# Gate projections by Strassen's seven products, w_out in 512-column halves, and two conditioning blocks in another order

## The chip, the cores and the metric

The kernel runs on one core of a Trainium2 chip. The metric is the device time of one execution in microseconds (us), the median of several runs. TensorE is called PE here, VectorE DVE, ScalarE ACT, GpSimd POOL, and SyncE SP. All DMAs of the kernel are issued from SP's queue.

## The reference

Two layers over 1024 latent tokens and 256 context tokens, each of width 1024. The change touches the projection of the gates `g`, the merge and the output projection:

```python
h = _rms(x) * (1.0 + scale) + shift               # scale, shift, gate: s_c @ w_ada[l] + b_ada[l]
fa, za, u, vs, zb, q, k, va, zc, g = _split_proj(h @ w_in[l])
# three mixers: Fourier (ya), gated spatial mixing (yb), windowed attention (yc)
ga, gb, gc = jnp.split(jax.nn.sigmoid(g), 3, axis=-1)       # each [tokens, 1024]
merged = ga * (ya @ w_pa) + gb * (yb @ w_pb) + gc * (yc @ w_pc)
x = x + gate * (merged @ w_out)
```

The context tokens go through the same layer with their own conditioning in layer 0, and give only keys and values in layer 1.

## The kernel before

**Numbers.** Every float32 product is made of three fp32r products: an operand is split into a high part (a cast on ACT, `whi`, `hh`) and a low part (a subtraction on DVE, `wlo`, `hl`), and `mm3` adds high times high, high times low and low times high in PSUM. So a projection of 128 output columns over 1024 inputs for one token group is 8 x 3 matmuls. Latents are in two groups of 512 tokens, "0" and "1"; the context is group "C" with 256. `H[g]` holds the normalised input of a group as eight [128, tokens] high and eight low tiles; later the same name holds the merged values.

**Stages of a layer.** Attention with side work; the Fourier mixer with the products of `w_pc`; spatial mixing (`sgu`) with the products of `w_pa` (`products`, results stored to DRAM as P); the gates; the output phase. Some gate blocks are computed ahead, in the stages before (`ahead`, results stored as T): four 512-token blocks in layer 0, eight in layer 1, besides those of the context.

**Gates (`gates`, L663 on).** For each of eight column blocks j and three branches b, one projection of 24 matmuls 512 wide for each latent group: 44 such blocks are left in layer 0, 40 in layer 1. The weights come as one [128, 8, 128] tile, cast (L212) and subtracted (L213) 1024 columns at a time. ACT takes the tanh, DVE forms (tanh + 1) * P (`add`, L673 and L676), POOL adds it to the merged tile M (L677). The products of `w_pb` are made in the same loop, into PSUM, and used from there. Merged latents go through DRAM; the merged context goes straight into `H["C"]`.

**Conditioning.** Next to the gates, DVE also multiplies rows of `w_ada` by the conditioning vectors and accumulates them (`ada_dve`, L192 and L196, 256 columns at a time): twelve items of two column blocks in layer 0, each 16 instructions, and four items of 8 instructions in layer 1. A tiny matmul (L200) sums over partitions.

**Output phase (`out_phase`).** For a token group, four quarters of `w_out` of 256 columns; for each, 24 matmuls per 128 tokens, then DVE multiplies by the gate (L927) and POOL adds to x (L929). Group order in layer 0: C, 0, 1. Then `modulate` prepares the next layer.

**Start.** Four blocks of layer 0's conditioning (`ada_rows`, 512 columns each): one at a time by eight fp32 matmuls on PE, and one with the sums on DVE.

**What sets the order.** The program is written in order with "fill" generators that place PE work between steps; a scheduler then moves instructions on each engine by its own timeline, and each engine runs its list strictly in that order.

Of the kernel before, what the change touches and what calls it, by code (L numbers as in the profile page):

```python
# [66 lines left out]
def trunk_kernel(ctx: ExitStack, tc: tile.TileContext, a: dict, out: bass.AP):  # L67
# [109 lines left out]
    def ada_dve(l, jb, nv, pool):  # L177

        raws = []
        for half in range(2):  # L180
            raw = pool.tile([128, 4, 256], F32, "araw", bufs=2)
            src = a["w_ada"][l, half * 512:(half + 1) * 512, jb * 128:jb * 128 + 256]
            nc.sync.dma_start(raw, src.rearrange("(k p) c -> p k c", p=128))
            raws.append(raw)

        def finish():
            acc = pool.tile([128, nv, 256], F32, f"aacc{nv}")
            for k in range(8):
                for v in range(nv):
                    sc = scol[:, k, v:v + 1]  # L190
                    if k == 0:
                        ins = DVE.tensor_scalar(acc[:, v, :], raws[0][:, 0, :], sc, None, ALU.mult)  # L192
                        if v == 0:
                            tc.keep_in_program_order(ins)
                    else:
                        DVE.scalar_tensor_tensor(acc[:, v, :], raws[k // 4][:, k % 4, :], sc, acc[:, v, :], ALU.mult, ALU.add)  # L196
            pa = bank("o")
            for i in range(2):
                for v in range(nv):
                    PE.matmul(pa[:, 2 * i + v:2 * i + v + 1], acc[:, v, i * 128:(i + 1) * 128], ones[:, 0:1], start=True, stop=True)  # L200
            for i in range(2):
                DVE.tensor_scalar(adac[l][:, jb + i, 0:nv], pa[:, 2 * i:2 * i + nv], bada[l][:, jb + i:jb + i + 1], None, ALU.add)

        return finish


    def granule(src, shape):
        raw = wp.tile(shape, F32, "raw", bufs=2)
        nc.sync.dma_start(raw, src)
        hi = wp.tile(shape, F32R, "whi", bufs=5)  # L210
        lo = wp.tile(shape, F32R, "wlo", bufs=5)
        ACT.copy(hi, raw)  # L212
        DVE.tensor_tensor(lo, raw, hi.bitcast(F32), ALU.subtract)  # L213
        return hi, lo

    def w_cm(l, c0):

        return granule(a["w_in"][l, :, c0:c0 + 128].rearrange("(k p) c -> p k c", p=128), [128, KC, 128])

    def w_tm(w, c0):  # L220

        r = []
        for half in range(2):
            src = w[half * 512:(half + 1) * 512, c0:c0 + 256].rearrange("(k p) c -> p k c", p=128)
            r.append(granule(src, [128, 4, 256]))
        return r
# [6 lines left out]
    def proj_cm(o, wg, h, n):  # L233

        for k in range(KC):
            mm3(o[:, :n], wg[0][:, k, :], wg[1][:, k, :], h[0][k], h[1][k], k == 0, k == KC - 1)

    def proj_tm(o, wt, h, t0):

        for k in range(KC):  # L240
            wh, wl = wt[k // 4]
            mm3(o[:, 0:256], h[0][k][:, t0:t0 + 128], h[1][k][:, t0:t0 + 128],
                wh[:, k % 4, :], wl[:, k % 4, :], k == 0, k == KC - 1)
# [324 lines left out]
    def side_work(l, groups, S, st):  # L568
# [40 lines left out]
        lead = context_blocks(range(9, 12)) if "C" in groups else [(b, 2, "0") for b in (0, 2)]  # L609
# [3 lines left out]
    def before_work(l, groups, S, st):  # L613
# [3 lines left out]
        return ahead(l, [(b, 1, "0") for b in (0, 2)], S, st, CTX)  # L617
# [23 lines left out]
    def products(l, groups, y, nkb, wname, b, S, st):  # L641

        per = 4 // nkb
        for j in range(8):
# [4 lines left out]
            for i, g in enumerate(groups, j):  # L649
                n = GROUPS[g][1]  # L650
                pp = bank("mm")
                for kb in range(nkb):
                    mm3(pp[:, :n], pg[0][:, kb, jo:jo + 128], pg[1][:, kb, jo:jo + 128],
                        y[g][0][:, kb, :], y[g][1][:, kb, :], kb == 0, kb == nkb - 1)
                s = staged(st, n)
                if i % 2:
# [6 lines left out]
    def gates(l, groups, S, ada, side, yb):  # L663

        mp = Pool(tc, name="mp", bufs=1, side=side)
        zq = Pool(tc, name="zq", bufs=1, side=side)
        lat = [g for g in groups if g != "C"]
        hC = new_h("C") if "C" in groups else None
        todo = []

        def add(m, b, t, n, pp):
            if b == 0:
                DVE.scalar_tensor_tensor(m, t, 1.0, pp, ALU.add, ALU.mult)  # L673
            else:
                s = tb(n)
                DVE.scalar_tensor_tensor(s, t, 1.0, pp, ALU.add, ALU.mult)  # L676
                POOL.tensor_tensor(m, m, s, ALU.add)  # L677

        def branch(b, j, g):
            return fetched(mp, S["P", b, j, g], GROUPS[g][1], 3, f"lp{b}")  # L680

        def sums():
            if todo:
                todo.pop()()
            if ada:
                todo.append(ada_dve(*ada.pop(0), zq))

        def product(j, g):
            n = GROUPS[g][1]
            pp = bank("pt")  # L690
            for kb in range(2):
                c = (j % 2) * 128
                mm3(pp[:, :n], pg[0][:, kb, c:c + 128], pg[1][:, kb, c:c + 128],
                    yb[g][0][:, kb, :], yb[g][1][:, kb, :], kb == 0, kb == 1)
            return pp[:, :n]

        for j in range(8):
            M = {g: mp.tile([128, GROUPS[g][1]], F32, "m" + g, bufs=2) for g in groups}
            W = {}
            if j % 2 == 0:  # L700
                raw = zq.tile([128, 2, 256], F32, "praw")
                nc.sync.dma_start(raw, a["w_pb"][l, :, j * 128:j * 128 + 256].rearrange("(k p) c -> p k c", p=128))
                pg = [zq.tile([128, 2, 256], F32R, f"p{x}") for x in "hl"]
                split(*pg, raw)
            if hC:
                for b in (0, 2, 1):
                    pp = branch(b, j, "C") if b != 1 else product(j, "C")
                    add(M["C"], b, fetched(mp, S["T", b, j, "C"], CTX, 2, "lt"), CTX, pp)
                ACT.activation(hC[0][j], M["C"], AF.Copy, scale=0.5)
                DVE.scalar_tensor_tensor(hC[1][j], M["C"], 0.5, hC[0][j].bitcast(F32), ALU.mult, ALU.subtract)  # L710
            order = [(b, g) for b in (0, 1, 2) for g in lat] if j < 7 else [(b, g) for g in lat for b in (0, 2, 1)]
            pb = {}
            for i, (b, g) in enumerate(order):
                n = GROUPS[g][1]
                if i == 2:
                    pb = {x: product(j, x) for x in lat}
                pp = branch(b, j, g) if b != 1 else pb.pop(g)
                if ("T", b, j, g) in S:
                    t = fetched(mp, S["T", b, j, g], n, 2, "lt")
                else:  # L720
                    if b not in W:
                        W[b] = w_cm(l, C_G + b * D + j * 128)
                    p = bank("mm" if g == "0" else "s")
                    proj_cm(p, W[b], H[g], n)
                    t = ta(n)
                    ACT.activation(t, p[:, :n], AF.Tanh, scale=0.5)
                add(M[g], b, t, n, pp)
                if i in (0, 4):
                    sums()
                if (b, g) == order[-1] or (g not in [x for _, x in order[i + 1:]]):  # L730
                    nc.sync.dma_start(stored(S, ("M", j, g), n), M[g])
        while todo or ada:
            sums()
# [385 lines left out]
```

## Time and profile before

| what | value |
|---|---|
| median of 3 runs | 1957.26 us (1956.96 to 1959.07) |
| the profiled execution, its own time | 1955.91 us |
| its span, first to last instruction | 1954.1 us |
| granted TensorE clock, mean | 0.992 |
| busy share: PE, DVE, ACT, POOL | 97%, 56%, 41%, 32% |
| matmuls 128x512 by 128x128 on L229 to L231, weights as `whi`, `wlo` | the largest group, 283.5 us of PE on L229 alone |
| DMA, mean | 133 GB/s, 41.7% of the 16 engines on SP's queue |

The page gives busy times; a PE instruction's own duration is longer than the distance to the next one, since matmuls overlap, so counts are priced by the distance between starts. The same holds for DVE. The stages can be told by the names of the tiles: a matmul `s<-hh,whi` is a gate block, `pt<-ybh,ph` a product of `w_pb`, `s<-whi,hh` one of the output phase. In time, layer 0's gates and `w_pb` products lie between 688 and 978 us, layer 1's between 1578 and 1834 us.

### The profile page before, as it was taken

How to read it: one execution, taken by the hardware profiler on the slowest of the kernel's cores; microseconds unless marked ns; L12 is line 12 of the kernel's file. 1: busy time of each engine (PE TensorE's matmuls, PEld its weight loads, DVE VectorE, ACT ScalarE, POOL GpSimd, SP SyncE). 2: the span in 40 equal slices, each digit the busy share in tenths (PEclk: the TensorE clock that was granted, in tenths of full speed). 3: DMA queues.
4: the chain of work that ended last, by engine and by line, in shares of the span. 5: the costliest groups of instructions: out<-in, count | busy, mean ns of one | idle time of the engine just before them, and what ended most of it. 6: DMA issues, size and time to landing. Idle time of an engine off the chain costs nothing.

```text
span 1954.1 us, 32830 instructions
## 1 busy us (share of the span) xinstructions
PE 1899.2 (97%) x11839; PEld 1686.4 (86%) x11839; DVE 1090.1 (56%) x2211; ACT 799.2 (41%) x2088; POOL 633.2 (32%) x1011
## 2 busy tenths in 40 slices
PE   7989999999999999999999989999999999999998
PEld 2888999999988887888899988899888788888898
DVE  4565665556655648766365456666565655522342
ACT  2654565455644422111243445655554443111320
POOL 1564444444231112211234544345433021211132
PEclk9999999999999999999999989999999999999999
DMA  8332122213555667554474321122124558532462
GB/s 312 120 99 66 49 67 64 68 48 103 163 181 164 194 222 227 170 175 132 151 250 144 108 66 58 57 61 79 33 87 154 165 186 277 185 105 80 140 222 86
DMA packets 280858, 259.89 MB, mean 133 GB/s; under 512 B 20792, under 2 KB 233976, under 8 KB 280696
## 3 DMA queue, kind: packets, MB, share of 16 engines
q1 hardware_dynamic: 280696, 257.80, 41.7%
q8 instruction: 93, 1.52, 0.3%
q14 instruction: 69, 0.57, 0.1%
HBM read 196.91 MB, written 60.83 MB: 132 GB/s over the span
## 4 chain that ended last, share of the span: by engine, by line
PE 84%; DMA 5%; DVE 4%; ACT 2%; issue 2%; POOL 1%; SPq 1%; POOLq 0%; DVEq 0%; ACTq 0%
PE mm L229 17%; PE mm L230 16%; PE mm L231 16%; PE s L230 6%; PE s L229 6%; PE s L231 6%; PE pt L391 3%; PE o L399 2%; PE o L398 2%; PE s L363 1%; PE s L356 1%; DMA lt<-dT 1%; PE s L166 1%; PE s L357 1%; DMA araw<-in_w_ada_dram 1%
## 5 line engine op out<-in xcount | busy, mean ns | idle before, releaser
L212 ACT CAST whi<-raw 128x1024 fp32r<-128x1024 f32 (+2 forms) x210 | 202.2, 966 | 388.1 <-PE s L230 144.0
L213 DVE TENSOR_TENSOR wlo<-raw,whi 128x1024 fp32r<-128x1024 f32 (+2 forms) x210 | 245.0, 1170 | 204.2 <-ACT whi L212 198.9
L229 PE MATMUL mm<-hh,whi 128*128 128x512 f32 (+1 forms) x752 | 293.6, 390 | 4.9 <-DVE st L554 2.7
L230 PE MATMUL mm<-hl,whi 128*128 128x512 f32 (+1 forms) x752 | 292.4, 389 | 0.0
L231 PE MATMUL mm<-hh,wlo 128*128 128x512 f32 (+1 forms) x752 | 291.8, 388 | 0.0
L229 PE MATMUL mm<-whi,hh 128*128 128x256 f32 x832 | 240.1, 289 | 5.4 <-DVE qt L439 2.5
L231 PE MATMUL mm<-whi,hl 128*128 128x256 f32 x832 | 238.3, 286 | 0.0
L230 PE MATMUL mm<-wlo,hh 128*128 128x256 f32 x832 | 237.2, 285 | 0.0
L677 POOL TENSOR_TENSOR m<-m,tb 128x512 f32<-128x512 f32 x64 | 87.5, 1370 | 409.3 <-DVE tb L676 365.9
L229 PEld LDWEIGHTS mm<-hh,whi 128*128 128x128 f32 x752 | 142.5, 189 | 32.9 <-DVE st L554 3.7
L229 PEld LDWEIGHTS mm<-whi,hh 128*128 128x128 f32 x832 | 160.8, 193 | 7.3 <-issue 2.9
L231 PEld LDWEIGHTS mm<-hh,wlo 128*128 128x128 f32 x752 | 142.4, 189 | 27.6
L230 PEld LDWEIGHTS mm<-hl,whi 128*128 128x128 f32 x752 | 142.6, 190 | 25.7
L230 PEld LDWEIGHTS mm<-wlo,hh 128*128 128x128 f32 x832 | 160.9, 193 | 0.1
L231 PEld LDWEIGHTS mm<-whi,hl 128*128 128x128 f32 x832 | 160.8, 193 | 0.2 <-DVE hl L284 0.2
L379 POOL TENSOR_SCALAR P<-P,rd 128x640 f32<-128x640 f32 (+2 forms) x144 | 113.2, 797 | 108.6 <-DVE rd L377 49.7
L230 PE MATMUL s<-hl,whi 128*128 128x512 f32 x352 | 137.5, 391 | 0.0
L229 PE MATMUL s<-hh,whi 128*128 128x512 f32 x352 | 137.4, 390 | 0.0
L231 PE MATMUL s<-hh,wlo 128*128 128x512 f32 x352 | 137.2, 390 | 0.0
L261 DVE TENSOR_TENSOR pl<-pt,ph 128x512 fp32r<-128x512 f32 (+1 forms) x184 | 111.8, 615 | 24.4 <-ACT ph L260 22.4
L260 ACT CAST ph<-pt 128x512 fp32r<-128x512 f32 (+1 forms) x184 | 95.8, 535 | 28.4 <-PE o L398 13.3
L196 DVE SCALAR_TENSOR_TENSOR aacc<-araw,scol,aacc 128x256 f32<-128x256 f32 x196 | 102.8, 558 | 4.9 <-DMA araw<-in_w_ada_dram 2.5
(303 smaller groups left out, 4640.9 us busy)
## 6 DMA issues: line engine op xcount, KB each, us to landing
raw<-in_w_in_dram SPq DMA_DIRECT2D x122, 512.0 KB, 4.0
araw<-in_w_ada_dram SPq DMA_DIRECT2D x48, 512.0 KB, 5.6
raw<-in_w_out_dram SPq DMA_DIRECT2D x40, 512.0 KB, 3.8
dP<-st SPq DMA_DIRECT2D x64, 256.0 KB, 2.3
lp<-dP SPq DMA_DIRECT2D x64, 256.0 KB, 4.2
x<-in_x_dram SPq DMA_DIRECT2D x16, 512.0 KB, 7.9
raw<-in_w_pc_dram SPq DMA_DIRECT2D x32, 256.0 KB, 2.8
dM<-m SPq DMA_DIRECT2D x32, 256.0 KB, 3.5
```

Source lines behind the costliest of these rows:

```text
L196: DVE.scalar_tensor_tensor(acc[:, v, :], raws[k // 4][:, k % 4, :], sc, acc[:, v, :], ALU.mult, ALU.add)
L212: ACT.copy(hi, raw)
L213: DVE.tensor_tensor(lo, raw, hi.bitcast(F32), ALU.subtract)
L229: PE.matmul(o, lh, rh, start=start, stop=False)
L230: PE.matmul(o, lh, rl, start=False, stop=False)
L231: PE.matmul(o, ll, rh, start=False, stop=stop)
L260: ACT.copy(hi, src)
L261: DVE.tensor_tensor(lo, src, hi.bitcast(F32), ALU.subtract)
L379: POOL.tensor_scalar(P[hh][:, :nl + 256], P[hh][:, :nl + 256], rd[:, hh:hh + 1], 1.0, ALU.mult, ALU.mult)
L391: PE.transpose(b[:, (2 * i + hh) * 128:(2 * i + hh + 1) * 128], P[hh][:, (i0 + i) * 128:(i0 + i + 1) * 128], ident)
L398: PE.matmul(po, vs, ph[:, i * 256:(i + 1) * 256], start=(i0 + i == 0), stop=False)
L677: POOL.tensor_tensor(m, m, s, ALU.add)
```

## The change

**Gates.** The gate projection of two neighbouring column blocks for both latent groups is written as a 2 x 2 matrix product: columns 2p and 2p+1 against the low and the high half of the 1024 inputs (a11, a12, a21, a22), and the two halves against the two token groups (B11 and B21 for group "0", B12 and B22 for group "1"). Strassen's form (with Winograd's sums) takes seven products of half depth for what took eight: 7 x 12 matmuls in place of 4 x 24. The four combinations of the token side, T1 = B12 - B11, T2 = B22 - T1, T3 = B22 - B12 and T4 = B21 - T2, are made once a layer in a new step, `differences`: for each of four tiles and each combination POOL subtracts the high parts, DVE subtracts the low parts and adds both, ACT and DVE split again. T1 overwrites B12. The weight side needs four sums per set (s1 to s4, two on DVE, two on POOL) and seven operand splits of 512 columns; the products accumulate on each other in three PSUM tiles, with copies to SBUF by ACT between, and adds on DVE and POOL after.

Layer 0 has one set of four blocks ahead and 11 sets in `gates`; layer 1 has two ahead and 10 in `gates`.

**What moves with it.** The `w_pb` products leave the gate loop and run before it, next to `differences`, stored to DRAM like the others and copied by ACT. Merged context values go through DRAM as well. The conditioning sums come in quarters, one after each product (`ada_steps`). The group order of layer 0's output phase becomes 0, C, 1, and the first six of eight input tiles of group "0" are merged before the last set ends.

**Output phase.** Two halves of `w_out` of 512 columns in place of four quarters of 256.

**Weights.** All weights are cast and subtracted 512 columns at a time, in ten buffers each in place of five of 1024.

**Start.** Of the four first conditioning blocks, block 12 instead of block 0 is now the one summed on DVE, and block 0 is done on PE right after block 8.

```diff
-    def ada_dve(l, jb, nv, pool):
+    def ada_steps(items, pool):
+        todo = []
+        def quarter(l, jb, nv, q, acc):
+            raw = pool.tile([128, 2, 256], F32, "araw", bufs=2)
...
+            def sums():
...
+                for k in range(2):
+                    for v in range(nv):
...
+                            ins = DVE.scalar_tensor_tensor(acc[0][:, v, :], raw[:, k, :], sc, acc[0][:, v, :], ALU.mult, ALU.add)
...
+    def operand(src, n=512):
+        hi = wp.tile([128, 512], F32R, "whi", bufs=10)[:, :n]
+        lo = wp.tile([128, 512], F32R, "wlo", bufs=10)[:, :n]
+        ACT.copy(hi, src)
+        DVE.tensor_tensor(lo, src, hi.bitcast(F32), ALU.subtract)
+        return hi, lo
...
+    def differences(tpool):
...
+        T2, T3, T4 = new("t2"), new("t3"), new("t4")
+        def steps():
+            for k in range(KC // 2):
+                for t, x, y in ((T3, B22, B12), (B12, B12, B11), (T2, B22, B12), (T4, B21, T2)):
+                    d = ta()
+                    POOL.tensor_tensor(d, x[0][k].bitcast(F32), y[0][k].bitcast(F32), ALU.subtract)
+                    e = tb()
+                    DVE.tensor_tensor(e, x[1][k].bitcast(F32), y[1][k].bitcast(F32), ALU.subtract)
+                    DVE.tensor_tensor(d, d, e, ALU.add)
+                    split(t[0][k], t[1][k], d)
+                    yield
...
+        def times(o, A, B, start):
+            for k in range(KC // 2):
+                c = slice(k * 128, (k + 1) * 128)
...
+                PE.matmul(o, A[0][:, c], B[0][k], ...)
+                PE.matmul(o, A[0][:, c], B[1][k], ...)
+                PE.matmul(o, A[1][:, c], B[0][k], ...)
+            next(sums, None)
...
+                z, y, x = bank("mm"), bank("s"), bank("pt")
+                A = operand(a11)
+                times(z, A, B11, True)
+                x1 = copy("x1", z)
+                s1 = combined(DVE, a21, a22, ALU.add)
+                A = operand(s1)
+                times(y, A, T1, True)
+                x5 = copy("x5", y)
+                s2 = combined(POOL, s1, a11, ALU.subtract)
+                A = operand(s2)
+                times(z, A, T2, False)
+                x2 = copy("x2", z)
+                A = operand(a12)
+                times(x, A, B21, True)
+                DVE.tensor_tensor(x1, x, x1, ALU.add)
+                merge(js[0], "0", x1)
+                s4 = combined(DVE, a12, s2, ALU.subtract)
+                s3 = combined(POOL, a11, a21, ALU.subtract)
+                A = operand(s3)
...
+                times(z, A, T3, False)
+                x3 = copy("x3", z)
+                def p3():
+                    A = operand(s4)
+                    times(y, A, B22, False)
+                    DVE.tensor_tensor(x2, y, x2, ALU.add)
+                    merge(js[0], "1", x2)
+                def p4():
+                    A = operand(a22)
+                    times(z, A, T4, False)
...
+                POOL.tensor_tensor(x3, x3, x5, ALU.add)
+                merge(js[1], "1", x3)
...
-            for n in range(4):
-                w = wt.pop(n) if n in wt else w_tm(a["w_out"][l], n * 256)
+            for n in range(2):
+                w = wt.pop(n) if n in wt else w_half(a["w_out"][l], n)
...
+    h0 = ada_rows(0, 0, sp)
...
-    ada_rows(0, 12, sp)()
     h0()
+    h1 = ada_rows(0, 12, sp, True)
     ada_rows(0, 4, sp)()
+    h1()
...
+        sevens, combos = differences(tpool)
+        fill = Fill(products(l, groups, yb, 2, "w_pb", 1, S, st, True))
...
+        gates(l, groups, S, ada, A, sevens)
```

**How the order moves.** Counted over the whole program, the matmuls go from 11757 to 10641: 252 of 512 columns are gone with the eighth product, and 1728 of 256 columns in the output phase have become 864 of 512. Three places in the listing of each engine's order follow; a row gives the source line, the operation, what it writes and reads (with the tile's number) and the shape of what it writes.

DVE in layer 0's gates, before: conditioning sums (`aacc2`), the low part of weights (`wlo`), the split of the `w_pb` weights (`pl`) and the merges (`m1`, `tb`).

```order
L673 SCALAR_TENSOR_TENSOR m1_10515<-ta_10633,lp0_10606 128x512
L261 TENSOR_TENSOR pl_10824<-praw_10821,ph_10823 128x512
L202 TENSOR_SCALAR adac1_90<-o_10595,bada1_92 128x2 x2
L192 TENSOR_SCALAR aacc2_10754<-araw_10602,scol_93 128x256
L196 SCALAR_TENSOR_TENSOR aacc2_10754<-araw_10602,scol_93,aacc2_10754 128x256 x3
L676 SCALAR_TENSOR_TENSOR tb_10683<-ta_10681,pt_10636 128x512
L196 SCALAR_TENSOR_TENSOR aacc2_10754<-araw_10604,scol_93,aacc2_10754 128x256 x4
L213 TENSOR_TENSOR wlo_11131<-raw_11128,whi_11130 128x1024
L676 SCALAR_TENSOR_TENSOR tb_10713<-ta_10711,pt_10643 128x512
```

In these nine rows one weight tile is split, and the merges read a product from PSUM (`pt`). The same engine and stage in the changed kernel: low parts of sums (from `sw`) and of weights (from `raw`), the adds that read a product from PSUM (L813, L829), a merge into `lp`, and conditioning sums (in `tb`).

```order
L193 TENSOR_SCALAR tb_10350<-araw_10292,scol_93 128x256 x2
L195 SCALAR_TENSOR_TENSOR tb_10235<-araw_10266,scol_93,tb_10235 128x256
L813 TENSOR_TENSOR x1_10462<-pt_10432,x1_10462 128x512
L195 SCALAR_TENSOR_TENSOR tb_10350<-araw_10292,scol_93,tb_10350 128x256 x2
L225 TENSOR_TENSOR wlo_10777<-sw_10774,whi_10776 128x512
L225 TENSOR_TENSOR wlo_10801<-sw_10772,whi_10800 128x512
L225 TENSOR_TENSOR wlo_10838<-raw_10653,whi_10837 128x512
L195 SCALAR_TENSOR_TENSOR tb_10350<-araw_10323,scol_93,tb_10350 128x256 x2
L766 SCALAR_TENSOR_TENSOR lp_10541<-x1_10462,lp_10541 128x512
L195 SCALAR_TENSOR_TENSOR tb_10350<-araw_10323,scol_93,tb_10350 128x256
L829 TENSOR_TENSOR x2_10515<-s_10431,x2_10515 128x512
```

The merge reads `lp` and the sum from SBUF, low parts of weight sums have come in, and an add that waits for a product (L813) stands ahead of the low parts of later products.

PE in layer 1's gates, before: gate blocks (`hh`, `hl` against `whi`, `wlo`) with the products of `w_pb` (`ybh`, `ybl` against `ph`, `pl`) set into the middle of one.

```order
L230 MATMUL mm_19759<-hl00_12298,whi_19755 128x512
L231 MATMUL mm_19759<-hh00_12296,wlo_19756 128x512
L229 MATMUL mm_19759<-hh00_12296,whi_19755 128x512
L229 MATMUL pt_19562<-ybh0_19021,ph_19544 128x512
L230 MATMUL pt_19562<-ybl0_19022,ph_19544 128x512
L229 MATMUL pt_19569<-ybh1_19023,ph_19544 128x512
L230 MATMUL pt_19569<-ybl1_19024,ph_19544 128x512
L231 MATMUL pt_19562<-ybh0_19021,pl_19545 128x512
```

In the changed kernel, at the start of layer 1's gates: the end of the first Strassen product (onto B11, `hh00`), the second, onto T1 (`hh01`, in the place of B12), and the third, onto T2 (`t2h`).

```order
L748 MATMUL mm_20290<-hl00_12435,whi_20293 128x512
L749 MATMUL mm_20290<-hh00_12433,wlo_20294 128x512
L747 MATMUL s_20291<-hh01_13139,whi_20315 128x512
L748 MATMUL s_20291<-hl01_13141,whi_20315 128x512
L747 MATMUL mm_20290<-t2h_19915,whi_20337 128x512
L748 MATMUL mm_20290<-t2l_19916,whi_20337 128x512
L749 MATMUL s_20291<-hh01_13139,wlo_20316 128x512
```

The products of `w_pb` are gone from here; all of them stand ahead of the first Strassen product, whose twelve matmuls are the only ones between them and the first matmul that reads a combination.

PE at the start of layer 0's output phase, before: the end of the last gate block and the first matmuls of 128 tokens.

```order
L229 MATMUL s_11314<-hh11_603,whi_11216 128x512
L230 MATMUL s_11314<-hl11_605,whi_11216 128x512
L231 MATMUL s_11314<-hh11_603,wlo_11217 128x512
L229 MATMUL s_11378<-whi_11364,hh0C_9102 128x256
L230 MATMUL s_11378<-wlo_11365,hh0C_9102 128x256
L231 MATMUL s_11378<-whi_11364,hl0C_9104 128x256
```

And in the changed kernel, the same place:

```order
L270 MATMUL mm_12126<-whi_12089,hh00_11949 128x512
L271 MATMUL mm_12126<-wlo_12090,hh00_11949 128x512
L747 MATMUL mm_11856<-t4h_9315,whi_11991 128x512
L748 MATMUL mm_11856<-t4l_9316,whi_11991 128x512
L749 MATMUL mm_11856<-t4h_9315,wlo_11992 128x512
```

An output matmul writes 512 columns in place of 256, and the first blocks, now of group "0", are begun before the last product of the gates.

More of the change, by code (lines that the diff above doesn't have):

```diff
@@ L616, in before_work @@
             return ahead(l, context_blocks(range(9)), S, st)
-        return ahead(l, [(b, 1, "0") for b in (0, 2)], S, st, CTX)
+        return ahead(l, [(0, j, "0") for j in range(2)], S, st, CTX)
     def few(gen, n):
@@ new lines, in gates, with merged, copy, combined @@
+    def gates(l, groups, S, ada, side, blocks):
+        mp = Pool(tc, name="mp", bufs=1, side=side)
+        B11, B21, B22, T1, T2, T3, T4 = blocks
+        sums = ada_steps(ada, mp)
+        lat = ("0", "1")
+        def merged(g, k, pool, tag, bufs):
+            m = fetched(pool, S["M", k, g], GROUPS[g][1], bufs, tag)
+            ACT.activation(H[g][0][k], m, AF.Copy, scale=0.5)
+            DVE.scalar_tensor_tensor(H[g][1][k], m, 0.5, H[g][0][k].bitcast(F32), ALU.mult, ALU.subtract)
+        S["merged"] = merged
+        def times(o, A, B, start):
+            for k in range(KC // 2):
+                c = slice(k * 128, (k + 1) * 128)
+                last = k == KC // 2 - 1
+                PE.matmul(o, A[0][:, c], B[0][k], start=start and k == 0, stop=False, skip_group_check=True)
+                PE.matmul(o, A[0][:, c], B[1][k], start=False, stop=False, skip_group_check=True)
+                PE.matmul(o, A[1][:, c], B[0][k], start=False, stop=last, skip_group_check=True)
+            next(sums, None)
+        def copy(tag, o):
+            x = mp.tile([128, 512], F32, tag)
+            ACT.copy(x, o)
+            return x
+        def combined(engine, x, y, op):
+            s = mp.tile([128, 512], F32, "sw", bufs=2)
+            engine.tensor_tensor(s, x, y, op)
+            return s
+        def add(m, b, t, pp):
@@ L674, in add @@
             else:
[L675 to L731, printed above, removed]
@@ L735, in gates @@
+        for k in (KC - 2, KC - 1):
+            merged("0", k, mp, "araw", 2)
         mp.close()
@@ L987, in trunk_kernel @@
         lat = ["0", "1"]
-        blocks = [(b, 0, g) for b in (0, 2) for g in lat]
+        blocks = [(b, j, "1") for b in (0, 2) for j in range(2)] if last else [(0, j, g) for j in range(2) for g in lat]
         half = len(blocks) // 2
```

213 lines of the change are left out of this document (141 added, 72 removed).

## The prediction

> **What bounds the kernel now.** I read the page first: shares by engine, then the chain that ended last.
>
> ```profile
> span 1954.1 us, 32830 instructions
> PE 1899.2 (97%) x11839; PEld 1686.4 (86%) x11839; DVE 1090.1 (56%) x2211; ACT 799.2 (41%) x2088; POOL 633.2 (32%) x1011
> ...
> PEclk9999999999999999999999989999999999999999
> ...
> PE 84%; DMA 5%; DVE 4%; ACT 2%; issue 2%; POOL 1%; SPq 1%; POOLq 0%; DVEq 0%; ACTq 0%
> ```
>
> PE works 97% of the span at a clock of 0.9 or more in all slices but one (0.8), and 84% of the chain lies on it. Matmuls taken away are worth their time, as long as no other engine then needs longer. The change takes them from two stages and puts DVE and POOL work into the same stages, so I asked for these two stretches (layer 0's gates and `w_pb`, layer 1's) by engine:
>
> ```profile
> core 0: us, PE busy (x) PEld busy (x) DVE busy (x) ACT busy (x) POOL busy (x), PEclk, DMA share, GB/s
> 688.00:978.00 290.00, 286.89 (x1335) 238.08 (x1335) 180.88 (x339) 62.97 (x96) 57.78 (x51) 1.00 0.58 178
> 1578.00:1834.00 256.00, 255.15 (x1137) 210.25 (x1136) 103.56 (x148) 60.62 (x91) 44.19 (x35) 1.00 0.48 153
> ```
>
> In both, PE has no gap worth naming (3.1 and 0.9 us), at full clock. In layer 0 DVE and POOL have 239 us of work in 290 us, in layer 1 148 in 256. What decides is what they will have.
>
> **Prices.** PE, from starts of matmuls inside one run of equal ones: 24 apart at 512 columns, 12 apart at 256.
>
> ```profile
> 962.09 0.39 PE L229 MATMUL s<-hh,whi 128*128 128x512 f32 x1
> ...
> 967.53 0.39 PE L229 MATMUL s<-hh,whi 128*128 128x512 f32 x1
> ...
> 984.16 0.28 PE L229 MATMUL s<-whi,hh0C 128*128 128x256 f32 x1
> ...
> 985.60 0.28 PE L229 MATMUL s<-whi,hh1C 128*128 128x256 f32 x1
> ```
>
> 5.44/24 = 0.2267 us and 1.44/12 = 0.120 us. DVE, from rows of several instructions back to back against a single one:
>
> ```profile
> 655.03 2.50 DVE L261 TENSOR_TENSOR yal<-sza,yah 128x512 fp32r<-128x512 f32 x4
> ...
> 765.12 0.60 DVE L192 TENSOR_SCALAR aacc<-araw,scol 128x256 f32<-128x256 f32 x2
> 769.54 0.48 DVE L196 SCALAR_TENSOR_TENSOR aacc<-araw,scol,aacc 128x256 f32<-128x256 f32 x1
> 769.94 0.69 DVE L673 SCALAR_TENSOR_TENSOR m<-ta,lp 128x512 f32<-128x512 f32 x1
> 770.54 2.46 DVE L196 SCALAR_TENSOR_TENSOR aacc<-araw,scol,aacc 128x256 f32<-128x256 f32 x6
> ```
>
> 512 columns with two operands: (2.50 - 0.69)/3 = 0.603. A conditioning step of 256: (2.46 - 0.48)/5 = 0.396. A `TENSOR_SCALAR` of 256: about 0.26 (0.60 for two, less the overlap). POOL, and what it does to DVE:
>
> ```profile
> 773.68 1.27 POOL L677 TENSOR_TENSOR m<-m,tb 128x512 f32<-128x512 f32 x1 [11.86 <-DVE tb L676]
> 781.80 1.46 POOL L677 TENSOR_TENSOR m<-m,tb 128x512 f32<-128x512 f32 x1 [6.85 <-DVE tb L676]
> ...
> 781.03 0.69 DVE L676 SCALAR_TENSOR_TENSOR tb<-ta,pt 128x512 f32<-128x512 f32 x1
> 781.63 2.31 DVE L196 SCALAR_TENSOR_TENSOR aacc<-araw,scol,aacc 128x256 f32<-128x256 f32 x3
> ```
>
> Three conditioning steps alone take 0.48 + 2 x 0.396 = 1.27 us; beside POOL's add at 781.80 they took 2.31. So 1.04 us of a POOL operation is taken from DVE when both read two operands from SBUF: the two do not overlap, they add. That is the rule I count with. A DVE operation that reads PSUM (`pt`, 0.69) shows no such lengthening.
>
> [...]
>
> **Layer 0's gates.** *PE.* Before: 44 blocks x 24 x 0.2267 = 239.4, `w_pb` 8 x (12 x 0.2267 + 6 x 0.120) = 27.5, conditioning's tiny matmuls about 5 (an estimate; the same before and after): 272, with the 3 of gaps 275 us. The remaining 15 of the window are its ends. After: 11 sets x 84 x 0.2267 = 209.5, + 27.5 + 5 = 242. So 30 us of matmuls go, with up to 3 of gaps.
>
> *DVE and POOL after.* Counted from the order of the changed kernel, from the first low-part difference to the output phase: 221 DVE operations on two 512-column operands in SBUF (differences, sums, low parts, merges) x 0.603 = 133; 168 conditioning steps x 0.396 = 67; 24 scalings x 0.26 = 6; together 206. POOL: 13 differences, 22 sums s2 and s3, 10 adds of x5 to x3, 36 merges = 81, x 1.04 = 84. As the two add, 290 us of work stands against 242 of PE. The 22 adds that read PSUM and 24 tiny operations (about 16) may run beside POOL: 290 to 307. The last 12 or so lie under the first output matmuls, which do not wait for them. So 278 to 295; I take 286, against 275 before: **+11**. Bounds: -33, when POOL costs DVE nothing and PE stays the bound at 242; +32, when all 307 are in line. In this layer the saving would be eaten by the sums it needs.
>
> **Layer 1's gates.** PE before: 40 x 24 x 0.2267 = 217.6, `w_pb` 8 x 12 x 0.2267 = 21.8, 2 of others: 241, with gaps 242. After: 10 x 84 x 0.2267 = 190.4, in all 214. DVE: 202 x 0.603 + 28 x 0.396 + 4 x 0.26 = 134 (conditioning is small here); POOL 75 x 1.04 = 78; 212, some 10 of them behind the last product. PE stays just longer. But its start waits: T1 is whole only after about 40 DVE and 12 POOL operations, 40 x 0.603 + 12 x 1.04 = 37 us, while PE has `w_pb` (21.8), one product of 12 (2.7) and a little more, 26.5. The second product waits 10 us; what waits behind it is the whole of PE's list. With 5 more for places where DVE and POOL are behind for a set, 229: **-13**. Bounds -27 (no wait) to +2 (wait and saturation twice as large, each).
>
> **Output phases.** 1728 x 0.120 = 207.4 becomes 864 x 0.2267 = 195.9: -11.5. Against it, the last block is 512 wide where these two are 256:
>
> ```profile
> 1949.22 0.43 DVE L927 TENSOR_TENSOR og<-mm,gb 128x256 f32<-128x256 f32 x1 [2.45 <-PE mm L231]
> 1949.72 0.72 POOL L929 TENSOR_TENSOR x<-x,og 128x256 f32<-128x256 f32 x1 [2.14 <-DVE og L927]
> ```
>
> At 0.69 and 1.27 they end 0.8 later; and a half of `w_out` takes 8 of the 10 weight buffers, so the next half is split late at a few group boundaries, some 0.7. **-10**, bounds -11.5 to 0. [...]
>
> **The start.** Block 0's rows on PE come right after those of block 8:
>
> ```profile
> 41.10 0.41 PE L171 MATMUL o<-ident,tb 2*128 2x2 f32 x4
> 41.76 0.41 PE L171 MATMUL o<-ident,tb 2*128 2x2 f32 x4 [0.26 <-DVE adac L172]
> 42.43 0.41 PE L171 MATMUL o<-ident,tb 2*128 2x2 f32 x4 [0.26 <-DVE adac L172]
> 43.08 0.89 PE L280 MATMUL pt<-ident,x 128*128 128x128 f32 x4 [0.25 <-ACT ta L282]
> ```
>
> The last three blocks end 0.66 apart just before the first transposes, so the order can move that point by about one or two such steps: **-1**. Bounds -4 to +2: several steps either way, the loads of 512 KB being the same.
>
> **At nothing.** ACT gets 24 copies of products of `w_pb` to SBUF, and three copies per set. SP gets their stores and loads:
>
> ```profile
> L657 ACT COPY st<-mm 128x512 f32<-128x512 f32 x32 | 18.6, 582 | 24.1 <-PE mm L231 20.5 <-issue 3.7
> ...
> dP<-st SPq DMA_DIRECT2D x64, 256.0 KB, 2.3
> lp<-dP SPq DMA_DIRECT2D x64, 256.0 KB, 4.2
> ```
>
> ACT is busy 63 of 290 us; 0.58 a copy, 14 + 19 us, leaves it under half. The loads land 4.2 us after issue and a set lasts 19 us (84 x 0.2267), so one set of lead covers them; without that cover a merge would be 4 us late, and DVE's list with it, 11 times: 46 us. They are issued through three buffers, ahead of use, and I charge nothing.
>
> **Sum.** The profiled execution took 1955.9 (span 1954.1 and 1.8 around it): + 11 - 13 - 10 - 1 = 1942.9. The median of the runs, 1957.26, lies 1.35 above it: **1944 us**.
>
> **Rivals.** (1) *PE stays the bound in both layers*: POOL's operations fall beside ACT work, DVE's waits and PSUM reads rather than beside two-operand DVE work, and the lock costs little. Then all 252 matmuls, 57.1 us, are gained: 1955.9 - 57.1 - 10 - 1 + 10 (layer 1's start) + 1.4 = 1899. For it: PE's 97%, and the 239 us of DVE and POOL in 290, which stalled PE hardly at all. Against it: 290 of such work in 242 of PE cannot be done without most of the overlap that 781.63 denies. 0.20.
>
> (2) *Slower: DVE waits for PE, and PE for DVE.* The adds that read a product in PSUM (L813, L829; 22 in layer 0, 20 in layer 1) stand in DVE's list ahead of the low parts of the next products. DVE stops at each until the product is done, conditioning and `wlo` queue behind it, and PE, having done the product, finds the next `wlo` missing: a split of 0.6, and the latency between, about 0.75 us each time. 42 of these cost 31 us on top of the forecast: 1975, slower than before. It decides once a set's DVE and POOL work exceeds the 19 us of its matmuls, since then no lead builds up; layer 0's 290/11 = 26 is above. For it: that order on DVE. Against it: ten weight buffers, two products of lead, and a DVE that is late doesn't wait at its adds. 0.20.
>
> (3) *The output phase doesn't deliver*: with 8 of 10 weight buffers in one half, each half is split late and PE waits away its 10 us: 1954.
>
> ```profile
> raw<-in_w_out_dram SPq DMA_DIRECT2D x40, 512.0 KB, 3.8
> ```
>
> For it: a load lands 3.8 us after issue and the splits follow. Against it: a half is used for 11 us (two runs of 24) or 22 (four). 0.06.
>
> [...] 0.08.
>
> **How the numbers follow.** The forecast case (DVE with POOL bound layer 0, PE layer 1) has 0.46 and its own range 1924 to 1964 (layer 0's work at 278 or 295 to 300, layer 1's start wait 0 or doubled). Beyond it lie case 1 around 1899 and case 2 around 1975; 1898 to 1976 cuts off about half of each, some 0.1 on either side. A difference of 0.2%, 4 us, is what measurement tells from none: 1953.3 to 1961.2. Faster: 0.38 of the forecast's 0.46, all of case 1 and 0.02 of case 3, 0.60. Same: 0.08 of the forecast's, 0.04 of case 3 and 0.03 of case 4, 0.15. Slower: case 2 and 0.05 of case 4, 0.25.
>
> **What would show it.** In layer 0's gates of the changed kernel PE should be busy about 242 of 286 us, its gaps ended by the low parts (`wlo`) on DVE, with DVE and POOL together near full and DVE's two-operand operations lengthened where a POOL operation lies over them. If PE is above 97% there, case 1 holds and the lock is overpriced; if DVE's own waits for products are large while PE also waits, case 2. In layer 1, one gap of about 10 us before the first matmul on T1 (written to B12's place), and PE near full after it. In the output phases starts 0.227 apart at 512 columns without gaps of several us at the halves. My number is wrong above all if POOL's operations find DVE idle or reading PSUM more often than I count.

## The result and the profile after

The changed kernel takes **2020.67 us** (median, 2018.56 to 2023.12), the kernel before 1957.91 beside it: a ratio of 1.0327, with an interval of 1.0307 to 1.0348. The forecast was 1944, range 1898 to 1976: the time lies outside, on the other side of before.

The page of the changed kernel, its first lines and its chain:

```profile
span 2018.3 us, 31865 instructions
PE 1883.4 (93%) x10723; PEld 1618.3 (80%) x10723; DVE 1357.2 (67%) x2572; ACT 933.9 (46%) x2473; POOL 781.5 (39%) x1062
...
PEclk9989999999999989989999999999999998889999
...
PE 38%; DVE 13%; DMA 5%; issue 4%; ACT 1%; POOL 1%; SPq 1%; POOLq 0%; DVEq 0%; ACTq 0%
```

PE does less and takes longer. The chain could be followed back only to 721 us here, so its shares add up to 63% of the span; of the part that it covers DVE has a fifth (13 of 63), where it had 4% before. The two stretches of Strassen's products, layer 0's and layer 1's, by engine (busy time and count; columns as before):

```profile
core 0: us, PE busy (x) PEld busy (x) DVE busy (x) ACT busy (x) POOL busy (x), PEclk, DMA share, GB/s
735.00:1025.00 290.00, 252.12 (x1043) 200.70 (x1042) 265.58 (x419) 100.70 (x182) 117.86 (x75) 0.92 0.61 184
1683.00:1923.00 240.00, 214.24 (x886) 170.41 (x885) 184.00 (x230) 97.31 (x172) 103.31 (x67) 0.93 0.54 158
```

In layer 0 DVE is busy 266 of 290 us and PE has 38 us without work; before, PE lacked 3. Where the time went, by the first start of a matmul of each stage in the two timelines (priced matmuls: counts by 0.2267 and 0.120 us):

| stage, from its first matmul to that of the next | before | after | change | of it priced matmuls |
|---|---|---|---|---|
| start, to layer 0's first query transposes | 76.2 | 71.4 | -4.8 | -2.2 |
| layer 0's attention, to the `w_pc` products | 501.8 | 505.1 | +3.3 | +2.4 |
| `w_pc` products and Fourier, to the `w_pa` products | 84.4 | 85.7 | +1.3 | -0.1 |
| `w_pa`, `w_pb`, gates, output phase, to layer 1's first query transposes | 461.3 | 505.1 | **+43.8** | -35.2 |
| layer 1's attention | 393.8 | 376.8 | -17.0 | -6.8 |
| `w_pc` products and Fourier | 70.5 | 77.3 | +6.8 | +3.6 |
| `w_pa` to the last matmul | 360.8 | 390.7 | **+29.9** | -30.3 |

So both stages that were to gain lost. For these two the forecast was 12 us less and the table has 74 more; the other stages give 10 back.

### The profile page after: what moved, and what is told of

Read it like the earlier page. It is cut to its first block, busy times and chain, and to the rows that moved or that the text cites. A ratio compares the mean times of both kernels' runs of the same rounds, so it can differ in the third digit from the quotient of the medians.

```text
span 2018.3 us, 31865 instructions
## 1 busy us (share of the span) xinstructions
PE 1883.4 (93%) x10723; PEld 1618.3 (80%) x10723; DVE 1357.2 (67%) x2572; ACT 933.9 (46%) x2473; POOL 781.5 (39%) x1062
## 4 chain that ended last, share of the span: by engine, by line
PE 38%; DVE 13%; DMA 5%; issue 4%; ACT 1%; POOL 1%; SPq 1%; POOLq 0%; DVEq 0%; ACTq 0%
PE mm L270 6%; PE mm L271 6%; PE mm L272 6%; DVE tb L195 4%; DVE wlo L225 3%; PE mm L747 2%; PE s L271 2%; PE s L270 2%; PE s L272 2%; PE mm L749 2%; PE mm L748 2%; PE pt L431 1%; DVE lp L766 1%; DMA raw<-in_w_in_dram 1%; PE s L749 1%
## 5 line engine op out<-in xcount | busy, mean ns | idle before, releaser
L225 DVE TENSOR_TENSOR wlo<-raw,whi 128x512 fp32r<-128x512 f32 (+1 forms) x363 | 272.2, 762 | 152.0 <-ACT whi L224 144.0
L224 ACT CAST whi<-raw 128x512 fp32r<-128x512 f32 (+1 forms) x363 | 220.3, 620 | 268.9 <-PE mm L271 85.7
L270 PE MATMUL mm<-whi,hh 128*128 128x256 f32 (+1 forms) x704 | 216.3, 307 | 5.8 <-DVE qt L479 2.8
L272 PE MATMUL mm<-whi,hl 128*128 128x256 f32 (+1 forms) x704 | 215.2, 306 | 0.0
L271 PE MATMUL mm<-wlo,hh 128*128 128x256 f32 (+1 forms) x704 | 214.7, 305 | 0.0
L270 PE MATMUL mm<-hh,whi 128*128 128x512 f32 (+1 forms) x432 | 167.4, 388 | 3.2 <-DVE qt L479 1.9
L272 PE MATMUL mm<-hh,wlo 128*128 128x512 f32 (+1 forms) x432 | 166.8, 386 | 0.0
L271 PE MATMUL mm<-hl,whi 128*128 128x512 f32 (+1 forms) x432 | 166.7, 386 | 0.0
L195 DVE SCALAR_TENSOR_TENSOR tb<-araw,scol,tb 128x256 f32<-128x256 f32 x196 | 135.3, 715 | 2.2 <-DMA araw<-in_w_ada_dram 2.1
L431 PE MATMUL pt<-ident,P 128*128 128x128 f32 x640 | 97.7, 272 | 0.0
```

Of the source, the lines that this page charges most:

```text
L195: ins = DVE.scalar_tensor_tensor(acc[0][:, v, :], raw[:, k, :], sc, acc[0][:, v, :], ALU.mult, ALU.add)
L224: ACT.copy(hi, src)
L225: DVE.tensor_tensor(lo, src, hi.bitcast(F32), ALU.subtract)
L270: PE.matmul(o, lh, rh, start=start, stop=False)
L271: PE.matmul(o, lh, rl, start=False, stop=False)
L272: PE.matmul(o, ll, rh, start=False, stop=stop)
```

## The experiments

Of the kernels below, "after" is the changed kernel with one or more edits, "before" the old one with a part of the change. Code left out is marked `...`.

**1. POOL's operations on DVE (after).**

```diff
-                    POOL.tensor_tensor(d, x[0][k].bitcast(F32), y[0][k].bitcast(F32), ALU.subtract)
+                    DVE.tensor_tensor(d, x[0][k].bitcast(F32), y[0][k].bitcast(F32), ALU.subtract)
...
-                s2 = combined(POOL, s1, a11, ALU.subtract)
+                s2 = combined(DVE, s1, a11, ALU.subtract)
```

(and likewise s3, the adds into M and x3 + x5)

> The changed kernel with all POOL operations of the differences, weight sums and merges (81 in layer 0, 75 in layer 1, two 512-column operands in SBUF each) done on DVE. Theory 'POOL and DVE add up': in layer 0 DVE loses about 74 us to POOL's operations (0.87 each) and would need 0.603 for each itself, so DVE gets 51 us of work and loses 74 us of delay: layer 0's stretch shorter by 20 to 50 us, layer 1's by 5 to 15, time 1960 to 1998. Rival 'DVE is short of throughput and POOL's share helps it': layer 0 longer by 40 to 50, time above 2050. Rival 'chains between engines, not throughput': within 10 us of 2020.

1973.7 us (one run): 47 less, with DVE doing all of POOL's work as well. The groups of DVE's instructions in layer 0's gates show why; first the changed kernel, then this one, columns busy time and mean duration in ns:

```profile
L195 DVE SCALAR_TENSOR_TENSOR tb<-araw,scol,tb 128x256 f32<-128x256 f32 x168 | 115.2, 714 | 1.3 <-DMA araw<-in_w_ada_dram 1.3
L225 DVE TENSOR_TENSOR wlo<-raw,whi 128x512 fp32r<-128x512 f32 x41 | 32.4, 791 | 2.4 <-ACT whi L224 2.3
```

```profile
L195 DVE SCALAR_TENSOR_TENSOR tb<-araw,scol,tb 128x256 f32<-128x256 f32 x168 | 77.7, 487 | 1.8 <-DMA araw<-in_w_ada_dram 1.8
L225 DVE TENSOR_TENSOR wlo<-raw,whi 128x512 fp32r<-128x512 f32 x42 | 28.9, 693 | 2.0 <-ACT whi L224 1.8
```

The same 168 conditioning steps take 37 us less when POOL is still. A POOL add took 1.50 us beside DVE, and the same add on DVE 0.70:

```profile
L767 POOL TENSOR_TENSOR m<-m,lp 128x512 f32<-128x512 f32 x31 | 46.6, 1504 | 72.3 <-DVE lp L766 72.3
```

```profile
L767 DVE TENSOR_TENSOR m<-m,lp 128x512 f32<-128x512 f32 x32 | 22.1, 697 | 0.0
```

POOL and DVE add up, as the theory said, and the rival that POOL's share helps is out. Where the time was gained is not as expected: 18.5 us in layer 0's stage and 22.6 in layer 1's last, for 20 to 50 and 5 to 15. In layer 1 the late weight load of experiment 3 is gone as well (the longest wait for raw weights is 4.0 us there), so not all of the 47 is POOL's direct share. Summed over DVE's timeline of the changed kernel from 700.4 to 1025.8 us (distance of each start to the next, less the undisturbed distance of that shape): 220 us undisturbed, 74 of lengthening, 30 idle. 85 POOL operations lie in it, so each cost DVE 0.87 us. Without POOL, from 695 to 968 us: 248, 1 and 22; behind the last product, from 968 to 994, another 20 us of DVE work follow.

**2. Conditioning sums on PE (after).** Eight fp32 matmuls with two rows per item of 256 columns in place of DVE's instructions.

```diff
-                            ins = DVE.scalar_tensor_tensor(acc[0][:, v, :], raw[:, k, :], sc, acc[0][:, v, :], ALU.mult, ALU.add)
...
+                    ins = PE.matmul(pr[0:2, 0:256], scol[:, 2 * q + k, :], raw[:, k, :], start=(q == k == 0), stop=(q == 3 and k == 1))
```

> The changed kernel with the conditioning sums beside the gates made by fp32 matmuls on PE (two rows, 256 columns) in place of 192 and 32 instructions on DVE. Theory 'layer 0 is bound by DVE with POOL': DVE loses about 72 us of its 294 in layer 0, PE gains some 25, so PE with about 270 becomes the longer one: time 1960 to 1985. Rival 'PE waits for chains of latency or for PE's own order': time 2020 to 2045, since PE only gets more work.

2020.2 us (one run): the time alone says the rival, the profile says that it was a bad exchange. Layer 0's gates and the new matmuls in them:

```profile
735.00:1025.00 290.00, 276.15 (x1158) 191.68 (x1157) 173.48 (x239) 102.66 (x182) 110.22 (x74) 0.98 0.60 183
...
L191 PE MATMUL o<-araw,scol 128*2 128x256 f32 x192 | 48.3, 389 | 6.8 <-DMA araw<-in_w_ada_dram 4.8 <-DVE adac L198 2.0
```

DVE's busy time fell from 266 to 173 us and PE's gaps from 38 to 14, but the sums cost PE 48 us, not the 25 that I had put: PE became the bound at the same length. Inconclusive as a test by time.

**3. The gate vector as rows (after).** `gate<-adac` writes 1024 elements of 4 bytes to DRAM. In layer 1 it went out between weight loads; SP's queue, then DVE:

```profile
1785.45 0.39 SPq L1011 DMA_DIRECT2D gate<-adac  x1
1785.89 0.58 SPq L231 DMA_DIRECT2D raw<-in_w_in_dram  x1
```

```profile
1784.99 0.68 DVE L766 SCALAR_TENSOR_TENSOR lp<-ta,lp 128x512 f32<-128x512 f32 x1
1798.88 0.69 DVE L759 TENSOR_TENSOR sw<-raw 128x512 f32<-128x512 f32 x1 [13.21 <-DMA raw<-in_w_in_dram]
```

DVE had nothing to do for 13.2 us, and PE then waited 9.1. The vector (4 KB) itself landed 11.7 us after its issue. The edit transposes it on PE first:

```diff
-            nc.sync.dma_start(row.rearrange("j p -> p j"), adac[l][:, 16:24, v])
...
+            PE.transpose(pg[0:8, 0:128], adac[l][:, 16:24, v], ident)
...
+            DVE.tensor_copy(rt[0:8, 0:128], pg[0:8, 0:128])
+            nc.sync.dma_start(row, rt[0:8, 0:128])
```

> The changed kernel with the gate vector written to DRAM as 8 rows of 512 bytes after a transpose on PE, in place of 1024 elements of 4 bytes. Theory 'the small-element transfer, issued between weight loads at 1785 us, holds up the weights behind it': the 13.2 us in which DVE waits for raw weights in layer 1 and the 9.3 us gap of PE behind it go, time 2007 to 2013. Rival 'the weights come late for another reason (a buffer that comes free late, SP's order)': within 4 us of 2020.

2005.45 us, ratio to before 1.0233 (1.0216 to 1.0250), 15 less than the changed kernel: more than expected. The wait of 13.2 is gone (the longest for raw weights there is now 3.9); the last stage is 7.6 us shorter, layer 0's stage 5.6. But in this kernel the transfer also goes out later, at 1895.1 us in layer 1, with the gates nearly done, where it had gone out at 1785.5, among their weight loads. Whether the rows or the later time removed the wait is not separated.

**4. The output phase alone (before).**

```diff
-            for n in range(4):
-                w = wt.pop(n) if n in wt else w_tm(a["w_out"][l], n * 256)
+            for n in range(2):
+                w = wt.pop(n) if n in wt else w_half(a["w_out"][l], n)
```

> The kernel before with the output phase by 512 columns and nothing else of the change. As the prediction had it (distance between starts): 11.5 us less of PE, 1.5 lost: time 1946 to 1949. Rival 'halves of w_out come late, four of five weight buffers each': time 1954 to 1960.

1948.75 beside 1959.64 us: ratio 0.994 (0.9925 to 0.9955), 10.9 less. This is the part of the change that does what it was priced at, and this kernel beats both.

**5. Layer 1's conditioning sums in layer 0's attention (after).** One 128-column block at a time, sixteen of them, one for every second step of the attention loop; the four items for layer 0's own gate stay in the gates.

```diff
-            ada += [(l + 1, j, 2) for j in range(0, 16, 2)]
...
         for u, (kv, g, t, pr) in enumerate(units):
+            if u % 2:
+                next(ahead_ada, None)
```

> The changed kernel with the conditioning sums for layer 1 (8 of the 12 items of layer 0's gates) done on DVE during layer 0's attention, 128 columns at a time; the four for layer 0's own gate stay. About 48 us of DVE work leaves layer 0's gates, with some of the delay by POOL that fell on it. Theory 'DVE with POOL bounds layer 0': DVE's line falls from 294 plus 30 of waits to about 245 plus waits, near PE's 242, so the stage is shorter by 35 to 50 and the time 1970 to 1990 (attention, with DVE 55 to 65% busy, taking up the work for 0 to 8). Rival 'chains of latency set the stage': within 10 us of 2020, or longer.

2038.14 us, ratio 1.0423 (1.0405 to 1.0441). Neither. Layer 0's products, from the first to the last matmul of Strassen's form, went from 290.8 to 267.3 us, but attention from 505.1 to 538.2: there DVE was busy 60% of the time before the edit (100 to 470 us) and 74% with it, and PE's busy time in that stretch fell from 362 to 344. That the bursts of sixteen instructions hold up other DVE work is my reading; it was not tested.

**6. Three edits: 1, 3 and 5 (after).**

> The changed kernel with three edits: POOL's operations on DVE, the gate vector as 8 rows of 512 bytes, layer 1's conditioning sums in layer 0's attention. If the three causes are separate: about 1974 (without POOL) less 9 to 15 (gate vector), less 22 (PE's wait for the last sums at the end of layer 0's gates without POOL): 1925 to 1945, and below the kernel before with the output phase by 512 columns (1949). If the chain of sums or PE's own order limits: 1955 or more.

1967.5 us, ratio 1.0057 (1.0041 to 1.0072). Attention again took 34 more (539.5); without them this kernel would be near 1933 (an estimate, 1967.5 - 34), where it was expected, but I had wrongly put attention's price at little.

**7, 8. The start alone, and the start with the output phase (before).**

```diff
-    h0 = ada_rows(0, 0, sp, True)
+    h0 = ada_rows(0, 0, sp)
...
-    ada_rows(0, 12, sp)()
-    h0()
+    h0()
+    h1 = ada_rows(0, 12, sp, True)
     ada_rows(0, 4, sp)()
+    h1()
```

> The kernel before with block 12 in place of block 0 summed on DVE at the start, nothing else. Prediction: 1 us less, between 4 less and 2 more. By the profile after (first transposes 3.4 us earlier, first keys 4.8): 3 to 5 less. Rival 'the later stages give it back' (the Fourier products of layer 0 began only 1.5 us earlier): 0 to 1.5 less.

> The kernel before with the output phase by 512 columns and the start of the change, without Strassen's form: the sum of the two, 11 and 1 to 5 less than before, 1941 to 1948.

The start alone: 1960.47 us, ratio 1.0016 (1.0007 to 1.0025). In its profile the first query transposes came 1.1 us earlier than in that of before, and attention was 5.3 longer. With the output phase: 1949.34, ratio 0.9963 (0.9948 to 0.9977), no better than the output phase alone. The gain at the start is given back in attention; why attention takes it, I did not find.

**9, 10. Weights by 512 columns, alone and with the output phase (before).**

```diff
-        hi = wp.tile(shape, F32R, "whi", bufs=5)
-        ACT.copy(hi, raw)
...
+        return [operand(raw[:, c:min(c + 512, n)], min(512, n - c)) for c in range(0, n, 512)]
```

> The kernel before with all weights cast and subtracted 512 columns at a time in ten buffers each in place of 1024 in five, and nothing else of the change. Prediction: nothing. Rival, from the stage between layer 1's first keys and its Fourier products, where the changed kernels took 377 us for 394 with only 7 us less of matmuls: finer splits save some of the other 10, time 5 to 10 below before.

> The kernel before with the output phase by 512 columns and the weights by 512 columns. If the two add up: 11 less than before from the output phase, and what the weights alone give.

Alone: 1961.55 us, ratio 1.0022 (1.0011 to 1.0034); with the output phase 1951.92, ratio 0.9975 (0.9963 to 0.9987). Layer 1's attention did become shorter, 385.6 for 393.8: this is half of the -17 in the table above, and the priced matmuls are 6.8 of it. But layer 0's stage of gates and output became 8.4 longer (469.7). I had put these splits at nothing; they cost about 4 alone, and about 7 beside the output phase (0.9975 for the 0.994 of experiment 4).

**11. The products of `w_pb` ahead of the gates (before).**

```diff
+        Fill(products(l, groups, yb, 2, "w_pb", 1, S, st)).rest()
         st.close()
...
-                pp = branch(b, j, g) if b != 1 else pb.pop(g)
+                pp = branch(b, j, g)
```

> The kernel before with the products of w_pb made ahead of the gates, stored and fetched again as in the change, the gates' form unchanged. Prediction: nothing, the moved copies and transfers being hidden. Rival 'the products need the gate blocks beside them as cover': in the changed kernels PE has 10 us of gaps in each layer's product stage, even without POOL: 8 to 20 more than before.

1975.81 us, ratio 1.0092 (1.0077 to 1.0107): 19 more, with not one matmul added. Of it 17.7 stand in layer 0's stage (479.0 for 461.3) and 1.9 in layer 1's last. PE's waits there, before and now (in all, times, longest):

```profile
PE o L200 <- DVE aacc L196: 1.9, 2, 1.1
PE mm L229 <- DVE st L659: 0.6, 1, 0.6
PE pt L231 <- DVE pl L261: 0.5, 1, 0.5
```

```profile
PE o L200 <- DVE aacc L196: 4.7, 3, 2.5
PE mm L229 <- DVE st L659: 3.6, 4, 1.8
PE s L229 <- ACT whi L212: 0.6, 3, 0.2
PE mm L229 <- ACT st L657: 0.5, 2, 0.3
```

Over the whole stage PE's gaps, those too short for the list with them, are 8.4 us more than before (11.7 for 3.3); steps between starts that are longer without a gap make another 8. The listed waits tell of two causes: a product that is stored needs its PSUM tile copied out before the next can use it (the rows with `st`, 4.1 us for 0.6), and the conditioning sums, with less time beside them, come late (4.7 for 1.9). The rest of the 19 is not put down to a cause.

**12. POOL's operations on DVE and the gate vector as rows (after).**

> The changed kernel with POOL's operations on DVE and the gate vector as 8 rows. If the two causes are separate: 46 and 15 less than 2020.7, 1955 to 1964. If the late weights only showed because DVE was late through POOL: 1966 to 1974.

1969.99 us, ratio 1.0058 (1.0040 to 1.0076): nearer the rival. The edit of experiment 3, worth 15 us by itself, is worth 4 on top of experiment 1 (a single run), where the longest wait for raw weights in layer 1 was already 4.0. What is left in layer 0 stands at the end of the gates (the products, then the wait behind them):

```profile
728.00:962.00 234.00, 224.76 (x1000) 181.42 (x999) 225.79 (x449) 98.24 (x172) 0.00 (x0) 0.99 0.65 203
962.00:988.00 26.00, 4.12 (x23) 3.94 (x22) 20.53 (x48) 4.50 (x9) 0.00 (x0) 0.59 0.63 208
```

DVE is full to the end, and behind the last product PE waits 22 us for conditioning sums that DVE had not reached. PE stands there because the one-column matmuls of these sums come ahead of the output phase in its list; a kernel with them further back was not run.

**13, 14. Layer 1's conditioning sums left out**, of the changed kernel and of kernel 12.

```diff
-            ada += [(l + 1, j, 2) for j in range(0, 16, 2)]
+            DVE.tensor_copy(adac[l + 1][:, 0:16, :], bada[l + 1][:, 0:16].unsqueeze(2).to_broadcast([128, 16, 2]))
```

> The changed kernel without the conditioning sums for layer 1 (8 of 12 items in layer 0's gates; layer 1 then runs on the biases alone, so the output is not the reference's). 48 us of DVE work is gone and comes back nowhere. Theory 'DVE with POOL bounds layer 0': 25 to 45 less than 2020.7. Rival 'chains between PE, ACT, DVE and POOL': within 10.

> The same left out of the changed kernel with POOL's operations on DVE and the gate vector as 8 rows (1970). Theory 'what remains in layer 0 is DVE's own throughput': DVE's line there falls from about 270 to 222, under PE's 242, so 30 to 42 less than 1970: 1928 to 1940. Rival 'the rest is lost elsewhere (the products' stage, layer 1)': 1950 to 1970.

1999.64 us, ratio 1.0209 (1.0193 to 1.0224): 21 less, between the theory's 25 and the rival's 10, 18.7 of it in layer 0's stage. And 1930.24, ratio 0.985 (0.9834 to 0.9866): 39.8 less than kernel 12, as the theory had it. The window behind the last product is gone:

```profile
728.00:962.00 234.00, 225.99 (x988) 182.06 (x987) 200.50 (x358) 102.84 (x184) 0.00 (x0) 0.99 0.62 192
```

PE is now the longer one, 226 of 234. These two kernels leave out work of DVE and, with it, two thirds of the one-column matmuls for which PE waited, so they do not tell DVE's load from PE's order.

**15. The same sums in layer 0's Fourier and spatial stages** (otherwise kernel 12).

> The changed kernel with POOL's operations on DVE, the gate vector as 8 rows, and layer 1's conditioning sums (128 columns at a time) in layer 0's Fourier and spatial stages, where DVE is about 55% busy, in place of attention. If those stages hide them: 1930 (sums left out) plus 0 to 10, below every kernel so far. If they cost what attention paid, 33: about 1963.

1985.51 us, ratio 1.0139 (1.0122 to 1.0155): worse than attention. The stage of `w_pc` and Fourier went from 86.8 in kernel 12 to 115.7, and layer 0's next stage is 467.5 where it was 444.7 with the sums left out. I found no place in layer 0 that takes these sums for nothing, and no kernel with Strassen's form that does the whole computation under the time before.

## Why the prediction was wrong, point by point

**Layer 0's gates: +11 forecast; this is the step that failed first.** The view was right (DVE with POOL sets the end, 290 of work against 242 of PE), and so was the work: 220 undisturbed, where I had 206 and 16 beside, and 74 of lengthening, where I had 84. What failed is the laying end to end: I took a list of work for a stage's length, 286. DVE's line ran 324, 49 above the 275 that the prediction had for before. Eight of the difference are the end, which did not lie under the output phase as I had assumed, and 30 are idle time of DVE, for which the sum had no term: 7.5 in the differences, where POOL, DVE and ACT wait in turn inside each of sixteen short chains, and 22 in the gates, 8.4 of that on two late `lp` loads. A bounding engine that waits for others is not full; I had looked at its work and not at its waits. One reading in the prediction had no ground in its row: the DVE operation on `pt` at 781.03 ended at 781.72, before POOL's began at 781.80, so it could not show whether reading PSUM spares it. The changed kernel shows it: the adds that read a product (L813, L829) took 0.68 us on average, as without POOL (0.69), and the four of the 22 that began under a POOL operation took 0.68 to 0.69. The scalings (L193), with one block from SBUF, are lengthened too, 0.64 for 0.36.

The wait for the conditioning sums shows on PE, in the changed kernel's layer 0 (waits, 734 to 984 us):

```profile
PE o L202 <- DVE tb L195: 20.8, 10, 7.4
PE s L747 <- ACT whi L224: 4.5, 2, 3.2
PE s L749 <- DVE wlo L225: 4.4, 4, 1.7
```

I had named `wlo` as what PE would wait for; more than half of the 38 us (20.8) was a matmul of one column that stands in PE's list and needs the sums, and everything behind it stood too.

**Layer 1's gates: -13 forecast, about +17 measured** (1657.4 to 1922.4 us, less 5.9 of output matmuls begun inside, 259; before 242 by the price). The wait at the start was about as large as forecast, gaps of 5.3 and 1.6 us for the 10, but by luck: PE did not wait for T1 there. T1's first tile had been split at 1642.5. What ended the longer gap was the cast of the first weight sum, which DVE had made late, behind the differences; ACT's row and PE's:

```profile
1690.67 0.62 ACT L224 CAST whi<-sw 128x512 fp32r<-128x512 f32 x1 [4.00 <-DVE sw L759]
1691.34 0.79 PE L747 MATMUL s<-hh,whi 128*128 128x512 f32 x1 [5.29 <-ACT whi L224]
```

T1's last tile was whole only at 1701.3, and PE had the fourth product to do until then. "5 more for places where DVE and POOL are behind" failed: from 1683 to 1923 PE was idle for 26 us (240 less 214 in the table above), and steps between starts that were longer without a gap made another 13, the clock being 0.84 to 0.89 up to 1810. Of the 26, 9.1 are the late weights behind the gate vector, which the prediction did not see at all, and 5.0 the conditioning; the other 5 are short waits for high and low parts of weights, while DVE was over 90% busy, from 1683 to 1770. From 1810 on PE is full, as forecast.

**The output phase: -10 forecast, 10.9 alone.** The price by starts (0.2267 us at 512 columns, 0.120 at 256) held. In the changed kernel it was given back: 4.0 us in layer 0 for a late low part, 5.7 in layer 1 because DVE lacked the gate vector. PE's rows with these waits:

```profile
1083.96 0.50 PE L271 MATMUL s<-wlo,hh0C 128*128 128x512 f32 x1 [4.03 <-DVE wlo L225]
```

```profile
1950.32 0.79 PE L270 MATMUL s<-whi,hh 128*128 128x512 f32 x1 [5.75 <-DVE og L1048]
```

**"At nothing": not so.** I priced the moved products by the busy time of ACT's copies and of SP's transfers. What they cost is 19 us in experiment 11, a part of it in waits of PE that had been covered before. How much of that stands in the changed kernel, where the differences lie beside the products, is not separated. The 512-column splits cost 4 more, or 7.

**The start: -1 forecast, +3 alone.** Too small to matter; the bounds of -4 to +2 missed it by little.

**The rivals.** (1) fell: PE lacked work for 38 of 290 us in layer 0's gates. (2) fell as a mechanism: DVE's waits at the two adds are 0.6 us in layer 0 in all, and 7.3 in layer 1, all after 1810, where PE is full. Its criterion (a set's DVE and POOL work above 19 us) was met, and what followed was the plain excess. (3) fell for the phase by itself, by experiment 4; of the two waits in the changed kernel, the 4.0 us for a late split are of its kind, the 5.7 are not. (4), a price of 1.27 us for each of POOL's operations, the whole duration in the row at 773.68, fell: an operation cost DVE 0.87 on average, less than my 1.04 too. The lengthening itself is there: in layer 0's gates of the changed kernel a conditioning step took 1.04 us where a POOL operation lay over it (71 of 168), 0.47 elsewhere. Some 12 us of POOL's operations lie over gaps of DVE, where they cost it nothing; by that, an estimate, one beside a working DVE costs (74 + 12)/85 = 1.01, close to the 1.04. The range left out what came because all cases shared one assumption, that a full DVE loses nothing.

## What to carry to other kernels

Price a transformation that trades matmuls for elementwise work by the engine that gets the work, and add that engine's waits in its busiest stage: a sum of durations is a lower bound of a stage, not its length (here 294 us of DVE's work ran 324). Where DVE is the bound, ask what an operation given to POOL costs it: here, with two SBUF operands, each took 0.87 us from DVE to save 0.60. And ask what PE did beside a product that is moved out of a loop: here its cover went with it, 19 us in experiment 11.

## What the runs showed that was not expected

- A 4 KB transfer of 4-byte elements landed after 11.7 us, and a 512 KB load issued 0.4 us behind it was there some 13 us after issue, where the median is 4.2. In the kernel before the transfer is as slow (11.2 in layer 1), and in layer 0 a load issued 3.2 us behind two of them landed after 11.5, without a gap on PE. For the transfer as rows no landing is on record.
- Of the windows here, the granted clock was lower in those in which PE had more gaps: 0.92 and 0.93 in the two windows above (38 us without work in 290, 26 in 240), 0.98 and 0.99 in layer 0's gates without POOL (17 in 243 in experiment 1, 9 in 234 in experiment 12), 1.00 before (3.1 in 290, 0.9 in 256). In layer 0's gates (735 to 1025 us) steps between starts that are longer without a gap before them add 20 us to the price, for 3 before: 66 of them are 0.38 to 0.50 us instead of 0.227. As DVE set that stage's end, it is not shown that they cost time there. That the gaps cause it was not tested.
